# First feed-forward product by seven products of halves, in blocks 2 to 4 of a hybrid decoder layer

## The chip, the cores and the metric

The kernel runs on one core of one Trainium2 chip. The metric is the device time of one execution in microseconds. A core has five engines that run side by side, each with its own queue in order: TensorE (PE; its weight loads are shown apart as PEld), VectorE (DVE), ScalarE (ACT), GpSimd (POOL) and SyncE (SP), which issues nearly all DMAs here.

## The reference, cut to what matters

One layer over 2048 tokens of width 1024: a token mixer (gated DeltaNet, 8 heads) and a memory attention (4 heads) in parallel, an output projection, a layer norm, then a squared-ReLU MLP of width 4096 and a second layer norm. The change is in the MLP and in how weights reach it.

```python
x = layer_norm(ALPHA * x + mix, ln1_g, ln1_b)
x = layer_norm(ALPHA * x + sqrelu_mlp(x, w_ff1, w_ff2), ln2_g, ln2_b)

def sqrelu_mlp(x, w1, w2):
    return jnp.square(jax.nn.relu(x @ w1)) @ w2
```

All of it is in float32.

## The kernel before, in words

**Precision.** A float32 operand of a large product is written as a high part (rounded to fp32r, a cast on ScalarE) and a low part (the difference, a subtraction on VectorE): `split`, lines 460 to 462. A product is then three matmuls, high x high, high x low and low x high: `mm3`, lines 478 to 481. Weights are split where they are used.

**Blocks.** The 2048 tokens go in four blocks of 512 (the loop of line 1135; blocks are counted from 1 in this document, b = 0 in the code is block 1). In a block come, in this order: the mixer's projections, the mixer of each head and the memory attention (lines 1151 to 1162); the output projection in three parts of four heads (`out_proj`, lines 1165 to 1198, called with k0 = 0, 8 and 4), the last of which ends each of the four chunks of 128 tokens with its layer norm and its transposition into Thi and Tlo (`norm1`, `to_T`); the MLP (`ff_seven`, lines 1014 to 1093), whose last group also starts the next block.

**The MLP.** The 4096 hidden rows go in four groups g. The first product takes, per group, eight weight tiles of 128 hidden rows (`ff1_tiles`, lines 1216 to 1222): 8 k x 3 matmuls of 512 tokens each, in the accumulator tile "af". The first four tiles of a block run in halves of 256 tokens, so that they can start when the first two chunks are transposed. ScalarE applies relu and square; VectorE makes four sums of the quarters of the hidden tile, and all of it is split into the "xh" and "xl" slots (lines 1040 to 1060). The second product is already done by seven products of halves (Strassen's scheme in Winograd's form, table `SEVEN`, line 1010): sums of the hidden tile's quarters times sums of w_ff2's quarters. The latter are made once, in block 1, by `keep_sums` (lines 994 to 1006) and kept in DRAM as `tsc`, unsplit.

**Weights.** A raw weight of 512 KB is loaded into one of three 4 KB slots a partition ("wraw") and split into one of four 8 KB slots ("whl", high and low beside each other; lines 464 to 508). The weights of the mixer's projections are kept split in DRAM (`wsc`) from block 1 on and later loaded so.

**The order.** Everything is recorded first (`Recorder.add`) with the operations that it depends on and an estimated duration (`cost`, lines 190 to 226). `issue` (lines 228 to 333) then simulates the five queues and one DMA stream and gives each engine the ready operation with the lowest number (`prio`, its place in the program plus `shift`). A tile gets its slot in the order in which tiles are first used. The emitted order is fixed; on the chip every engine keeps to it. Each instruction stands under line 333, where the recorder emits it, so the profile is read by tile names.

Of the kernel before, what the change touches and what calls it, by code (L numbers as in the profile page):

```python
# [14 lines left out]
P = 128  # L15
TB = 512
# [123 lines left out]
class Recorder:  # L140
    def __init__(self, nc, tc):
        self.nc, self.tc, self.ops, self.shift = nc, tc, [], 0
# [9 lines left out]
    def add(self, eng, fn, name, args, kw):  # L152
        o = Op()
        o.i, o.eng, o.fn, o.args, o.kw = len(self.ops), eng, fn, args, kw
        o.succ, o.npred, o.ready, o.extra = [], 0, 0, 0
        o.prio = o.i + self.shift
        wr = [v for k, v in kw.items() if k in ("out", "accum_out")]
        rd = [v for k, v in kw.items() if k not in ("out", "accum_out")]
        rest = list(args)
        if "out" not in kw and rest:  # L160
            wr.append(rest.pop(0))
        rd += rest
        wr = [v for v in wr if isinstance(v, Ref)]
        rd = [v for v in rd if isinstance(v, Ref)]
        o.dur = self.cost(o, name, wr, rd, args, kw)
        o.p0 = tuple(r.p0 for r in wr[:1] + rd[:1])
        preds = {}
        for refs, is_w in ((rd, False), (wr, True)):
            for r in refs:
                for q, qw, qk in r.buf.log:  # L170
                    if (is_w or qw) and (qk is None or r.keys is None or qk & r.keys):
                        preds[q.i] = q
        for refs, is_w in ((rd, False), (wr, True)):
            for r in refs:
                log = r.buf.log
                if is_w:
                    log[:] = [e for e in log if not (e[2] == r.keys or r.keys is None)]
                log.append((o, is_w, r.keys))
        for q in preds.values():
            q.succ.append(o)  # L180
        o.npred = len(preds)
        o.bufs = list({id(r.buf): r.buf for r in rd + wr}.values())
        for b in o.bufs:
            if b.first is None:
                b.first = o.i
            b.users += 1
        self.ops.append(o)
# [162 lines left out]
def hybrid_layer(  # L350
# [39 lines left out]
    NW, NR = 4, 3  # L390
# [62 lines left out]
    inv = {}  # L453
    for n, f in (("LB", P), ("XB", P), ("L32", P), ("X32", P), ("X64", P), ("L64", P), ("Q", 64)):
        inv[n] = rec.buf(cst, (P, 2, f), F32, n, 1, n)
        nc.gpsimd.memset(inv[n], 0.0)
# [7 lines left out]
    def pair():  # L464

        t = rec.buf(wp, (P, 2 * 1024), F32R, "whl", NW, "whl")
        return t, t[:, :1024].part(*range(KT)), t[:, 1024:].part(*range(100, 100 + KT))

    def hilo(src, eng=None):
        t, hi, lo = pair()  # L470
        split(src, hi, lo, eng)
        return t, hi, lo
# [10 lines left out]
    def load_cols(w, u, eng=None):  # L483

        rt = rec.buf(wp, (P, 1024), F32, "wraw", NR, "wraw")
        nc.sync.dma_start(out=rt, in_=w[u])
        return as_cols(*hilo(rt, eng)[1:])
# [3 lines left out]
    def load_in(b, u):  # L491

        if b == 0:
            rt = rec.buf(wp, (P, 1024), F32, "wraw", NR, "wraw")
            nc.sync.dma_start(out=rt, in_=w_in[u])
            t, hi, lo = hilo(rt)
            nc.sync.dma_start(out=wsc[u], in_=t.bitcast(F32))
        else:
            t, hi, lo = pair()
            nc.sync.dma_start(out=t.bitcast(F32), in_=wsc[u])  # L500
        return as_cols(hi, lo)

    def load_rows(w, u, nh):

        rt = rec.buf(wp, (P, 1024), F32, "wraw", NR, "wraw")
        nc.sync.dma_start(out=rt, in_=w[u, nh])
        hi, lo = hilo(rt)[1:]
        return hi.rearrange("p (k f) -> p k f", k=2), lo.rearrange("p (k f) -> p k f", k=2)
# [6 lines left out]
    def layer_norm(y, g, b, dst=None):  # L515
# [8 lines left out]
        nc.gpsimd.tensor_tensor(out=rs, in0=ve, in1=mhalf[:, 0:1], op=ALU.pow)  # L524
        for i in range(2):
            c = slice(i * 512, (i + 1) * 512)
            yi = y[:, c].part(i)
            nc.vector.scalar_tensor_tensor(out=yi, in0=yi, scalar=mv[:, 0:1], in1=g[:, c],
# [18 lines left out]
    def T_tiles():  # L547
        return (rec.buf(tp, (P, KT, TB), F32R, "Thi", 1, "Thi"),
                rec.buf(tp, (P, KT, TB), F32R, "Tlo", 1, "Tlo"))

# [7 lines left out]
    def memory():  # L558
# [14 lines left out]
        for h in range(MH):  # L573
            w = load_cols(w_mem_k, h)
# [8 lines left out]
        for kk in range(4):  # L583
            w = load_rows(w_mem_v, kk, 0)
# [403 lines left out]
    def raw_rows(src):  # L988
        rt = rec.buf(wp, (P, 1024), F32, "wraw", NR, "wraw")
        nc.sync.dma_start(out=rt, in_=src)  # L990
        hi, lo = hilo(rt)[1:]
        return hi.rearrange("p (k f) -> p k f", k=2), lo.rearrange("p (k f) -> p k f", k=2)
# [16 lines left out]

    SEVEN = (("A11", "B11", "A", False, (0, 0)), ("S3", 3, "C", False, (1, 1)), ("S2", 2, "A", True, (1, 0)),  # L1010
# [3 lines left out]
    def ff_seven(b, ff1_tiles, relu2, add, norm2):  # L1014
        Q = 2 * P
        for g in range(NS):
# [3 lines left out]
            for v in range(2):  # L1020
                lo = [slot("xl", "s%d" % v, F32R) for _ in range(7)]
                hi = [slot("xh", "d", F32R) for _ in range(7 if v == 0 else 4)]
                if v:
                    hi += [hq[:, 0].part(0), hq[:, 1].part(1), slot("xh", "on", F32R)]
                sqs = [None, None]
                fs = [8 * g + 2 * v + o for o in (0, 4, 1, 5)]
                for part in ((0, 1, 2, 3),) if g == 0 and v == 0 else ((0,), (1,), (2,), (3,)):
                    if b == 0:
                        for j in range(2):
                            if 2 * j in part:  # L1030
                                keep_sums(u0 + v, j)
                    for i, a in zip(part, ff1_tiles([fs[i] for i in part], len(part) > 1)):
# [7 lines left out]
                        st = tok_tile("ss4")  # L1040
                        a11, a21, a12, a22 = (sq[:, q * Q:(q + 1) * Q] for q in range(4))
                        s = [st[:, q * Q:(q + 1) * Q].part(q // 2) for q in range(4)]
                        sub = lambda o, x, y, op=ALU.subtract: nc.vector.tensor_tensor(out=o, in0=x, in1=y, op=op)
                        sub(s[0], a21, a22, ALU.add)
                        sub(s[1], s[0], a11)
                        sub(s[2], a11, a21)
                        sub(s[3], a12, s[1])
                        h3, l3 = hi[3 * j:3 * j + 3], lo[3 * j:3 * j + 3]
                        two = lambda ap: ap.rearrange("p (i f) -> p i f", i=2)
                        split(sq.rearrange("p (j i f) -> p i j f", j=2, i=2)[:, 0], two(h3[0]), two(l3[0]))  # L1050
                        h22 = hi[6][:, j * Q:(j + 1) * Q].part(("x", j))
                        l22 = lo[6][:, j * Q:(j + 1) * Q].part(j)
                        split(a22, h22, l22)
                        for q in range(2):
                            split(st[:, q * TB:(q + 1) * TB].part(q), h3[1 + q], l3[1 + q])
                        x = {"A22": (h22, l22)}
                        for q, (n0, n1) in enumerate((("A11", "A12"), ("S1", "S2"), ("S3", "S4"))):
                            x[n0] = h3[q][:, :Q], l3[q][:, :Q]
                            x[n1] = h3[q][:, Q:], l3[q][:, Q:]
                        X[2 * v + j] = x  # L1060
# [5 lines left out]
            for n, (xn, wn, bn, on, (th, nh)) in enumerate(SEVEN[i] for i in order):  # L1066
# [4 lines left out]
                def part(t, v):  # L1071
                    if w[v] is None:
                        w[v] = raw_rows(tsc[u0 + v, wn] if wn in (1, 2, 3, 4)
                                        else w_ff2[u0 + v + (0 if wn == "B11" else 2), 1 if wn == "B22" else 0])
# [21 lines left out]
    def first_tokens():  # L1096
        T = T_tiles()
        rt = rec.buf(wp, (P, KT, P), F32, "wraw", NR, "wraw")
        wt, hi, lo = pair()
        hi, lo = hi.rearrange("p (k f) -> p k f", k=KT), lo.rearrange("p (k f) -> p k f", k=KT)  # L1100
# [12 lines left out]
        nc.sync.dma_start(out=wsc[0], in_=wt.bitcast(F32))  # L1113
# [21 lines left out]
    for b in range(NB):  # L1135
# [12 lines left out]
        for i in range(12):  # L1148
            cat_slot(i)
        r, A = {}, {}  # L1150
        for t in range(H + 2):
# [9 lines left out]
            if b == 0 and t == 0:  # L1161
                memory()
        ys = [None] * NC

        def out_proj(k0, tail=None):
# [11 lines left out]
            def part(t, nh, tag):  # L1177
                a = bank("ao", tag)
                for u in range(2):
                    if (u, nh) not in ws:  # L1180
                        ws[u, nh] = load_rows(w_out, k0 // 2 + u, nh)
# [12 lines left out]
            else:  # L1194
                for t in range(NC):
# [8 lines left out]
        T1 = T_tiles()  # L1204

        def norm1(t):
            layer_norm(ys[t], g1, b1)
            to_T(ys[t], T1[0], T1[1], t)
# [7 lines left out]
        def ff1_tiles(fs, halves):  # L1216

            wa = [(load_cols(w_ff1, f), bank("af", "m" if halves and i == 3 else "acc")) for i, f in enumerate(fs)]
            for t0, n in ((0, 256), (256, 256)) if halves else ((0, TB),):
                for w, a in wa:  # L1220
                    project(a[:, t0:t0 + n], w, T1, n, t0)
            return [a for _, a in wa]

# [14 lines left out]
        ff_seven(b, ff1_tiles, relu2, add, norm2)  # L1238
# [56 lines left out]
```

## Time and profile before

| | us |
|---|---|
| median of three runs | 2916.93 (2912.59 to 2917.21) |
| the profiled execution | 2914.94 |
| its span | 2913.2 |
| PE busy | 2862.8 |
| DVE busy | 2191.8 |
| ACT busy | 1527.1 |

The granted TensorE clock is 0.996 over the span. The profile gives busy time and idle time by engine and tile, the chain of work that ended last, and the DMA rate; it can be asked for any stretch of the span. Block 2 runs from about 785 to 1490 us, block 3 to about 2205 us; the MLP of block 2 begins at 1143.8 us.

### The profile page before, as it was taken

What the parts mean: (1) busy time and instruction counts of PE and PEld (TensorE: products, weight loads), DVE (VectorE), ACT (ScalarE), POOL (GpSimd) and SP (SyncE); (2) the same over time, 40 slices, a digit from 0 to 9 for tenths busy, and PEclk for the clock granted to TensorE, in tenths of its full rate; (3) what the DMA queues carried; (4) which work ended last, traced back from release to release, by engine and by line L of the source; (5) the groups of instructions that cost most, each with busy time, mean ns of one, the idle gap of its engine ahead of it and who ended that gap; (6) DMA issues with size and microseconds to landing.
All of it is one profiled execution on the core that took longest, in us unless ns stands there. A gap on an engine that the chain in (4) does not pass through costs nothing.

```text
span 2913.2 us, 42812 instructions
## 1 busy us (share of the span) xinstructions
PE 2862.8 (98%) x14404; PEld 2382.0 (82%) x14404; DVE 2191.8 (75%) x5762; ACT 1527.1 (52%) x3678; POOL 428.3 (15%) x1033
## 2 busy tenths in 40 slices
PE   8999999999999999999999999999999999999998
PEld 7888778888788878888878887888887888788886
DVE  7999987666888886665688887756668888676667
ACT  6677625454456653555536665344454666444443
POOL 2333210000133311000023321000001332000000
PEclk9999999999999999999999999999999999999999
DMA  7655567555743332544473333344456332234444
GB/s 278 251 201 203 191 228 236 190 193 182 266 151 139 122 105 81 159 143 134 157 256 138 138 116 105 92 147 145 152 176 226 141 138 98 98 94 151 146 145 137
DMA packets 127708, 469.79 MB, mean 161 GB/s; under 512 B 14464, under 2 KB 16896, under 8 KB 109056
## 3 DMA queue, kind: packets, MB, share of 16 engines
q1 hardware_dynamic: 126912, 467.00, 47.8%
q8 instruction: 114, 1.87, 0.3%
q14 instruction: 106, 0.87, 0.1%
q10 hardware_dynamic: 576, 0.06, 0.0%
HBM read 402.97 MB, written 64.03 MB: 160 GB/s over the span
## 4 chain that ended last, share of the span: by engine, by line
PE 81%; DVE 10%; DMA 4%; ACT 3%; issue 1%; POOL 1%; SPq 0%; ACTq 0%; POOLq 0%; DVEq 0%
PE af L333 39%; PE ao L333 7%; PE az L333 5%; PE av L333 5%; PE ak L333 5%; PE aq L333 4%; PE amq L333 3%; DVE y L333 3%; PE pc L333 3%; PE po L333 2%; DVE whl L333 2%; PE pkq L333 1%; PE pq L333 1%; PE pp L333 1%; DMA wq<-in_w_ff_dram 1%
## 5 line engine op out<-in xcount | busy, mean ns | idle before, releaser
L333 DVE TENSOR_TENSOR whl<-wraw,whl 128x1024 fp32r<-128x1024 f32 (+1 forms) x446 | 541.3, 1217 | 449.5 <-ACT whl L333 447.8
L333 PE MATMUL af<-Thi,whl 128*128 128x512 f32 (+1 forms) x2304 | 649.9, 366 | 5.1 <-DVE whl L333 3.9
L333 ACT CAST whl<-wraw 128x1024 fp32r<-128x1024 f32 (+1 forms) x446 | 466.8, 1047 | 355.3 <-PE af L333 208.6
L333 PEld LDWEIGHTS af<-Thi,whl 128*128 128x128 f32 x2304 | 416.6, 189 | 75.9 <-DVE whl L333 4.8
L333 PE MATMUL af<-whl,xh 128*128 128x512 f32 x1536 | 472.2, 390 | 0.0
L333 PE MATMUL af<-Tlo,whl 128*128 128x512 f32 (+1 forms) x1152 | 421.0, 366 | 0.0
L333 PE MATMUL af<-whl,xl 128*128 128x512 f32 x896 | 347.0, 390 | 2.3 <-DVE xl L333 2.3
L333 PEld LDWEIGHTS af<-whl,xh 128*128 128x128 f32 x1536 | 288.8, 188 | 61.2 <-ACT xh L333 0.5
L333 PE MATMUL ao<-whl,ch 128*128 128x512 f32 x768 | 253.2, 401 | 1.2 <-DVE y L333 1.2
L333 PEld LDWEIGHTS af<-Tlo,whl 128*128 128x128 f32 x1152 | 217.2, 189 | 35.1
L333 POOL TENSOR_SCALAR ve<-mv 128x1 f32<-128x1 f32 x34 | 22.5, 663 | 1513.6 <-DVE mv L333 1509.7
L333 ACT ACTIVATE rl<-af 128x512 f32<-128x512 f32 x128 | 76.5, 598 | 272.1 <-PE af L333 270.1
L333 PEld LDWEIGHTS af<-whl,xl 128*128 128x128 f32 x896 | 168.5, 188 | 37.7 <-DVE xl L333 2.8
L333 PE MATMUL aq<-Thi,whl 128*128 128x512 f32 x512 | 184.4, 417 | 6.8 <-ACT Thi L333 6.8
L333 PE MATMUL ak<-Thi,whl 128*128 128x512 f32 x512 | 175.9, 402 | 0.0
L333 PE MATMUL az<-Thi,whl 128*128 128x512 f32 x512 | 174.9, 402 | 0.0
L333 PE MATMUL av<-Thi,whl 128*128 128x512 f32 x512 | 174.5, 403 | 0.0
L333 PEld LDWEIGHTS ao<-whl,ch 128*128 128x128 f32 x768 | 142.6, 188 | 27.8 <-DVE y L333 2.1
L333 PE MATMUL ao<-whl,cl 128*128 128x512 f32 x384 | 154.8, 404 | 0.0
L333 DVE SCALAR_TENSOR_TENSOR y<-y,af 128x512 f32<-128x512 f32 x224 | 146.5, 679 | 8.9 <-PE af L333 8.9
L333 PEld LDWEIGHTS aq<-Thi,whl 128*128 128x128 f32 x512 | 94.1, 191 | 20.0 <-ACT Thi L333 6.8
L333 PEld LDWEIGHTS az<-Thi,whl 128*128 128x128 f32 x512 | 95.4, 188 | 17.0
(257 smaller groups left out, 5814.2 us busy)
## 6 DMA issues: line engine op xcount, KB each, us to landing
wraw<-in_w_ff_dram SPq DMA_DIRECT2D x224, 512.0 KB, 4.2
whl<-wsc SPq DMA_DIRECT2D x108, 1024.0 KB, 4.8
wraw<-tsc SPq DMA_DIRECT2D x128, 512.0 KB, 3.3
wsc<-whl SPq DMA_DIRECT2D x36, 1024.0 KB, 5.4
wraw<-in_w_out_dram SPq DMA_DIRECT2D x48, 512.0 KB, 3.6
wraw<-in_w_in_dram SPq DMA_DIRECT2D x35, 512.0 KB, 6.3
wq<-in_w_ff_dram SPq DMA_DIRECT2D x64, 256.0 KB, 4.2
tsc<-wq SPq DMA_DIRECT2D x64, 256.0 KB, 3.5
```

What stands on the lines that cost most here:

```text
L333: o.fn(*[res(a) for a in o.args], **{k: res(v) for k, v in o.kw.items()})
```

## The change

**The first product in blocks 2 to 4** (`ff1_quads`) takes eight groups v of 512 hidden rows. Of w_ff1's part for such a group, [1024 x 512], and of the block's tokens, [1024 x 512], it makes halves in both directions and computes seven products (table `FF1_SEVEN`), each as 2 x 4 x 3 matmuls of 256 tokens. The accumulators are read after each product, by copies on ScalarE and additions on VectorE, then relu, square, sums and splits as before. Block 1 keeps the plain product.

**The tokens' halves.** `to_quads` takes the place of `to_T` in these blocks: the last part of the output projection takes the chunks in the order 2, 3, 0, 1; B11 and B21 come from chunks 2 and 3, and when chunks 0 and 1 are there, VectorE makes T1 to T4 from both, which are split too. T1 lies in two weight slots.

**Weight parts in DRAM.** In block 1, the split quarters A11, A12 and A22 of w_ff1 are stored (`keep_parts`, 96 DMAs of 256 KB) and later loaded split; the sums S1 to S4 are made on VectorE (`ff1_sums`, 128 subtractions or additions of 256 columns) and stored unsplit (128 DMAs of 128 KB). The split w_out is stored too (`osc`) and loaded split in blocks 2 to 4. Three of four quarters of w_ff2 that the second product reads directly are copied within DRAM during block 1's mixer (`copy_rows`, 24 DMAs of 512 KB, each held until the operation recorded before it: `nc.after`) and read from the copies.

**One ring of slots.** Raw weights, high parts and low parts each take one 4 KB slot of eleven ("w", shown as wr, wh and wl). Where a weight isn't needed raw any more, it is loaded into its low part's slot and split in place (`hilo_in`).

**Also:** six tiles of the mixer's triangular inverse go from fixed memory to slots that are zeroed anew in each block; the hidden tile's splits go in smaller pieces, A11 and A22 first (`put`); `layer_norm` gets a variant that no call uses. The core of the diff:

```diff
-    NW, NR = 4, 3
+    NW = 11
...
+    def hilo_in(src):
+        t = unit("wl")
+        hi, lo = unit("wh").part(*HI), t.part(*LO)
+        nc.sync.dma_start(out=t.bitcast(F32), in_=src)
+        split(t.bitcast(F32), hi, lo)
+        return hi, lo
...
+    def load_hilo(src):
+        hi, lo = unit("wh").part(*HI), unit("wl").part(*LO)
+        for i, r in enumerate((hi, lo)):
+            nc.sync.dma_start(out=r.bitcast(F32), in_=src[:, 1024 * i:1024 * (i + 1)].part(i))
+        return hi, lo
...
+        Q["T1"] = [[unit("Tx", (P, 4, 256))] for _ in range(2)]
+        Q["T2"] = [[rec.buf(tp, (P, 4, 256), F32R, "kq1", 1, "Tx")],
+                   [rec.buf(tp, (P, 1, 256), F32R, "inv", 6, "Tx") for _ in range(4)]]
...
+    def to_quads(y, Q, keep, t):
...
+            if t >= 2:
+                quad_split(Q, ("B11", "B21")[j], t, pts[j])
+                f = v4(slot("tf", "d"))
+                nc.scalar.copy(out=f, in_=pts[j])
+                keep[t, j] = f
+        if t < 2:
+            nc.shift = 200 if t == 0 else 130
...
+            sub(s["T1"], b12, keep[t + 2, 0])
+            sub(s["T2"], b22, s["T1"])
+            sub(s["T3"], b22, s["B12"])
+            sub(s["T4"], keep[t + 2, 1], s["T2"])
+            quad_split(Q, "T2", t, s["T2"])
...
+    def copy_rows(u):
+        nc.after = nc.ops[-1]
+        for n in ("B11", "B21", "B22"):
+            nc.sync.dma_start(out=fcp[u, n], in_=w_ff2[u + (0 if n == "B11" else 2), 1 if n == "B22" else 0])
+        nc.after = None
...
+    FF1_SEVEN = (("A11", "B11", "A", False), ("A12", "B21", "B", False), ("S2", "T2", "A", True), ("S3", "T3", "C", False),
+                 ("S1", "T1", "A", True), ("A22", "T4", "C", True), ("S4", "B22", "A", True))
...
+    def keep_parts(f, hi, lo):
+        g, o = f // 8, f % 8
+        v, i = 2 * g + (o % 4) // 2, o % 2
+        for n, k in (("A11", 0), ("A12", 1)) if o > 3 else (("A22", 1),):
+            for h, r in enumerate((hi, lo)):
+                c = 1024 * h + 512 * i
+                nc.sync.dma_start(out=fhl[v, n][:, c:c + 512].part(h), in_=r[:, 512 * k:512 * (k + 1)].bitcast(F32))
...
+    def ff1_sums(f):
...
+            for n, x, y, op in (("S1", c1, c2, ALU.add), ("S3", a1, c1, ALU.subtract), ("S2", s["S1"], a1, ALU.subtract),
+                                ("S4", a2, s["S2"], ALU.subtract)):
+                nc.vector.tensor_tensor(out=s[n], in0=x, in1=y, op=op)
+                nc.sync.dma_start(out=fsc[v, n][:, 512 * j + 256 * i:512 * j + 256 * i + 256].part(2 * j + i), in_=s[n])
...
-                for t in range(NC):
+                for t in (2, 3, 0, 1) if b else range(NC):
...
+        def ff1_quads(vs, ACs, Bs, put):
...
+                wn, tn, bn, on = FF1_SEVEN[n]
+                if wn[0] == "A":
+                    hi, lo = load_hilo(fhl[v, wn])
+                else:
+                    hi, lo = hilo_in(fsc[v, wn])
...
+                    for k in range(4):
+                        th, tl = quad_k(T1, tn, k)
+                        for m, (a, x) in enumerate(((hi, th), (hi, tl), (lo, th))):
+                            first = start and k == 0 and m == 0
+                            nc.tensor.matmul(o.part(keys, other) if first else o.part(keys), a[:, i, k], x, start=first,
+                                             stop=k == 3 and m == 2, skip_group_check=True)
```

The first two products of the first two groups of a block are put ahead of the others in `ff1_quads`, since they need B11 and B21 only.

More of the change, by code (lines that the diff above doesn't have):

```diff
@@ new lines, in quad_split @@
+    def quad_split(Q, c, t, src):
+        h = t % 2
+        cols = slice(h * P, (h + 1) * P)
+        sub = []
+        for hl in range(2):
+            k = 0
+            for i, r in enumerate(Q[c][hl]):
+                n = r.shape[1]
+                sub.append((hl, k, n, r[:, :, cols].part((c, hl, h))))
+                k += n
+        his = [x for x in sub if x[0] == 0]
+        for _, k, n, r in his:
+            nc.scalar.copy(out=r, in_=src[:, k:k + n])
+        for _, k, n, r in sub:
+            if r not in [x[3] for x in his]:
+                for _, kh, nh, rh in his:
+                    a, b = max(k, kh), min(k + n, kh + nh)
+                    if a < b:
+                        nc.vector.tensor_tensor(out=r[:, a - k:b - k], in0=src[:, a:b], in1=rh[:, a - kh:b - kh].bitcast(F32),
+                                                op=ALU.subtract)
@@ L986, in hybrid_layer @@
            for g in range(NS) for u in (4 * g, 4 * g + 1) for i in range(1, 5)}
[L988 to L992, printed above, removed]
+    fcp = {(u, n): rec.buf(dr, (P, 1024), F32, "fcp%d_%s" % (u, n), 1, "fcp")
+           for g in range(NS) for u in (4 * g, 4 * g + 1) for n in ("B11", "B21", "B22")}
+    def copy_rows(u):
[3 more added lines that the diff above has]
+        nc.after = None
     def keep_sums(u, j):
```

289 lines of the change are left out of this document (227 added, 62 removed).

## The prediction

> **What bounds the kernel now.** I read the page first, then the matmuls by shape, then the waits on the chain, then stretches of block 1 (the first) and block 2, then the DMA rate.
>
> ```profile
> span 2913.2 us, 42812 instructions
> PE 2862.8 (98%) x14404; PEld 2382.0 (82%) x14404; DVE 2191.8 (75%) x5762; ACT 1527.1 (52%) x3678; POOL 428.3 (15%) x1033
> ...
> PE af L333 39%; PE ao L333 7%; PE az L333 5%; PE av L333 5%; PE ak L333 5%; PE aq L333 4%; PE amq L333 3%; DVE y L333 3%; PE pc L333 3%; PE po L333 2%; DVE whl L333 2%; PE pkq L333 1%; PE pq L333 1%; PE pp L333 1%; DMA wq<-in_w_ff_dram 1%
> ```
>
> TensorE is busy 98% of the span, and the tile "af", the accumulators of both feed-forward products, is 39% of the chain that ended last. A busy PE alone proves little, since matmuls overlap; so the stretches:
>
> ```profile
> core 0: us, PE busy (x) PEld busy (x) DVE busy (x) ACT busy (x) POOL busy (x), PEclk, DMA share, GB/s
> 20.00:30.00 10.00, 10.00 (x44) 8.28 (x45) 9.93 (x29) 5.15 (x10) 1.88 (x5) 1.00 1.01 418
> 80.00:90.00 10.00, 10.00 (x46) 8.26 (x45) 9.44 (x31) 5.67 (x9) 1.10 (x3) 1.00 1.03 414
> 340.00:480.00 140.00, 133.60 (x728) 111.97 (x726) 110.61 (x208) 58.91 (x124) 12.79 (x20) 1.00 0.68 227
> 520.00:560.00 40.00, 40.00 (x179) 33.10 (x178) 22.79 (x38) 20.97 (x33) 0.00 (x0) 1.00 0.56 182
> ...
> 1175.00:1300.00 125.00, 125.00 (x553) 103.52 (x552) 77.64 (x108) 62.03 (x84) 0.00 (x0) 1.00 0.47 144
> ```
>
> The last row lies in the feed-forward part of block 2: 553 matmuls of 128x512 in 125 us, no idle PE, granted clock 1.00, VectorE 62% busy, DMA at 144 GB/s. So there a matmul of 512 columns costs 125 / 553 = 0.226 us of the span, and only fewer TensorE columns shorten it. The pace of 256 columns is in the trace too, since the first four tiles of a block run in halves (timeline of PE):
>
> ```profile
> 1155.08 0.28 PE L333 MATMUL af<-Tlo,whl 128*128 128x256 f32 x1
> 1155.20 0.40 PE L333 MATMUL af<-Thi,whl 128*128 128x256 f32 x2
> ...
> 1161.56 0.28 PE L333 MATMUL af<-Tlo,whl 128*128 128x256 f32 x1
> ```
>
> One Tlo matmul and two Thi matmuls repeat every 0.36 us: 18 rounds from 1155.08 to 1161.56, 54 matmuls in 6.48 us, 0.120 us each, a little over half of 0.226.
>
> **TensorE in blocks 2 to 4.** Before, a block's first product is 32 tiles x 8 k x 3 matmuls; 28 tiles are 672 matmuls of 512 columns, four tiles are 192 of 256 columns: 672 x 0.226 + 192 x 0.120 = 151.9 + 23.0 = 174.9 us. After, eight groups x 7 products x 2 x 4 x 3 = 1344 matmuls of 256 columns: 161.3 us. That is 13.6 us less in a block and 40.8 us in three. One eighth of the columns goes (21.9 us), and the halves' worse pace gives part back. Transposes into the accumulators (8 banks a block) stay as many. This term is on the path, because nothing else ends a wait in the stretch above.
>
> **Feeding these products.** A weight is now used up in 24 x 0.120 = 2.9 us, formerly in 24 x 0.226 = 5.4 us. The second product already lives with 12 x 0.226 = 2.7 us a weight, with the same splits, in the same stretch without idle PE. Four of seven weights are still split on ScalarE and VectorE, as four of four before; three come as finished high and low parts, which doubles their bytes. Per block the first product loads 24 x 1.05 + 32 x 0.52 = 41.9 MB instead of 16.8 MB; the stretch's 144 GB/s becomes about 144 + 25.1 / 0.33 ms = 220 GB/s, half of the 418 seen. VectorE by its rows:
>
> ```profile
> L333 DVE TENSOR_TENSOR whl<-wraw,whl 128x1024 fp32r<-128x1024 f32 x443 | 539.7, 1222 | 449.1 <-ACT whl L333 447.4
> L333 DVE TENSOR_TENSOR xl<-ss,xh 128x512 fp32r<-128x512 f32 x96 | 61.8, 684 | 0.0
> L333 DVE TENSOR_TENSOR ss<-sq 128x256 f32<-128x256 f32 x128 | 48.2, 418 | 0.0
> L333 ACT CAST xh<-ss 128x512 fp32r<-128x512 f32 x96 | 59.4, 622 | 49.5 <-DVE ss L333 49.5
> ```
>
> For each of 32 blocks of hidden rows come three more additions of 256 (PSUM in; taken at 0.418 us) and one more split piece, about 1.4 us; a group of 81 us holds four, so 62% of 125 us becomes about 75% of a shorter stretch. ScalarE gives its 512-wide pairs up for 11 pieces of 256 and was 50% busy. The w_out splits (12 x 1.222 us) leave blocks 2 to 4; VectorE was not the limit there, so that is worth nothing. The single ring of eleven 4 KB slots replaces three raw slots and four 8 KB pairs, the same 44 KB; a split weight that is loaded into its own low slot takes two slots instead of three, and two slots are lent to T1 for the whole feed-forward part: 9 / 2 = 4.5 weights in flight, formerly three raw and four split. I take zero, covered by the idle 38% of VectorE and the DMA's margin; without that cover a stall shows as PE waiting on "wl".
>
> **The start of the first product in blocks 2 to 4.** Here work is added just where little covers it:
>
> ```profile
> 1143.55 0.39 PE L333 MATMUL ao<-whl,cl 128*128 128x512 f32 x1
> 1143.78 0.28 PE L333 MATMUL af<-Thi,whl 128*128 128x256 f32 x1
> ...
> 1149.09 0.50 PE L333 MATMUL af<-Thi,whl 128*128 128x256 f32 x2 [0.93 <-DVE whl L333]
> ...
> 1153.02 0.60 PE L333 MATMUL pt<-ident,y 128*128 128x128 f32 x4
> 1153.38 0.36 PE L333 MATMUL af<-Thi,whl 128*128 128x256 f32 x1
> 1153.58 0.28 PE L333 MATMUL af<-Tlo,whl 128*128 128x256 f32 x1
> 1153.70 0.60 PE L333 MATMUL pt<-ident,y 128*128 128x128 f32 x4
> ```
>
> The last out-projection matmul starts at 1143.55, and the last token chunk is transposed at 1153.02 to 1154.1, some 10 us later. The four half tiles cover that: 96 x 0.120 = 11.5 us. After, chunks 2 and 3 come first, and the first two products of two groups need only them: 4 x 24 x 0.120 = 11.5 us of cover again. Then product S2 x T2 needs the last chunk after two subtractions on VectorE (0.68 each by the xl row of 512 columns), a cast on ScalarE (0.62 by the xh row) and four splits of 128 columns (0.3 each, an estimate from 0.418 for 256): 10.5 + 1.4 + 0.6 + 1.2 = 13.7 us against 11.5 + 1.1 us of transposes: 1 us short, if VectorE is free. It is not quite:
>
> ```profile
> 1147.82 1.21 DVE L333 TENSOR_TENSOR whl<-wraw,whl 128x1024 fp32r<-128x1024 f32 x1
> 1148.95 0.68 DVE L333 TENSOR_TENSOR Tlo<-pt,Thi 128x512 fp32r<-128x512 f32 x1
> 1149.55 0.20 DVE L333 BATCH_NORM_AGGREGATE mv<-bn 128x2 f32<-128x12 f32 x1
> 1149.66 1.17 DVE L333 TENSOR_TENSOR whl<-wraw,whl 128x1024 fp32r<-128x1024 f32 x1
> 1150.75 1.41 DVE L333 SCALAR_TENSOR_TENSOR y<-y,mv,l1g 128x512 f32<-128x512 f32 x2
> ```
>
> These follow each other without a gap. Four weight splits (4.8 us) leave this stretch, since the first four weights arrive split; for each of chunks 0 and 1 come four subtractions and three more splits, 2 x 7 x 0.68 = 9.5 us. Behind a late VectorE instruction queue the weight splits and accumulator reads of the next five products. Net 4.7 us of VectorE at worst lands on the path: bounds 0 (all of it behind later products) and 8 us (that plus the 1 us and two weight splits). I take 3 us less the 0.93 us that goes: 2 us a block, 6 us in all.
>
> **Block 1 pays for the stores.** It keeps its plain first product and gains these DMAs: 12 w_out weights x 2 x 0.52 = 12.6 MB; 96 pieces of 256 KB of split w_ff1, 25.2 MB; 128 pieces of 128 KB of its sums, 16.8 MB, made by 128 additions of 0.418 us on VectorE. The first product of one group is 8 x 24 x 0.226 = 43.4 us and receives 10.5 MB of that, 242 GB/s on top of the 182 GB/s of the row 520 to 560: 424 GB/s, where 418 is the best that any stretch shows. VectorE there rises from 22.8 of 40 us (57%) to about 88%. The first 140 us (row 340 to 480) hold 31.8 MB and get 12.6 + 10.5 MB: 54.9 MB, 392 GB/s. SyncE issues all of it in order, 0.33 us and more each:
>
> ```profile
> 454.54 2.03 SPq L333 DMA_DIRECT2D wraw<-in_w_ff_dram  x2
> 460.33 1.52 SPq L333 DMA_DIRECT2D tsc<-wq  x3
> 462.67 0.33 SPq L333 DMA_DIRECT2D wraw<-in_w_ff_dram  x1
> ```
>
> A store that waits for its sum holds up the weight loads queued behind it, and a raw slot stays taken until the sums have read it. Lower bound 0 (418 GB/s reached, the rest moved into the second product's quieter stretches). Upper bound: at the rate per share of the row 340 to 480, 227 / 0.68 = 334 GB/s, three groups take 18.4 / 0.334 = 55 us instead of 43.4 and the first stretch 164 instead of 140: 3 x 11.7 + 24 = 59 us. I take 3 us a group, 12 us, near the lower end, because the rows at 414 and 418 GB/s also mix stores with loads.
>
> **Copies of w_ff2 in block 1's first stage.** 24 copies, DRAM to DRAM, 12.6 MB read and written. The stretch from 100 to 340 us (its columns: us, PE busy, clock, DMA share, GB/s):
>
> ```profile
> 100.00:340.00 240.00, 238.23 (x1334) 1.00 0.56 198
> ```
>
> 198 GB/s becomes 198 + 25.2 / 0.24 = 303 GB/s: hidden on average, but a load behind a burst of three lands later. I take 3 us, bounds 0 and 10. Six memsets a block on GpSimd (15% busy) cost nothing.
>
> **The sum.** The profiled execution took 2914.9 us (span 2913.2 plus 1.7). 2914.9 - 40.8 + 6 + 12 + 3 = 2895 us. The median of the shown runs lies 2 us above that execution: 2897 us. A measurement of this kernel can tell about 0.2%, 6 us, from no change.
>
> **Rivals.**
> 1. All additions hide: 2916.9 - 40.8 - 2 (the small stall goes too) = 2874 us. For it: a planner that knows durations orders everything and PE is idle only 50 us now. Against it: DMA and VectorE demands near full in block 1.
> 2. Slower: block 1's first product becomes bound by DMA. The mechanism is the 424 GB/s of demand; it decides as soon as block 1 loses over 32 us (40.8 less the 9 us above), that is at a sustained rate of about 365 GB/s: there a group takes 50.4 us (7 more) and the first stretch 150 (10 more). At the bound of 334 GB/s: 2916.9 - 40.8 + 9 + 59 = 2944 us. For it: stores of 128 and 256 KB, in order on one queue. Against: 414 GB/s.
> The Trainium skill, "DMA: Bandwidth & Descriptors", section Specifications, states a limit of about 358 GB/s of HBM for one core; by that rule the groups cost 3 x 8 and the first stretch 13 us, 37 us in all, and the time is 2922 us. The rows at 414 and 418 GB/s do not agree with it as a limit here.
> 3. VectorE is late at each start by 8 us, or halves run slower than 0.120 us (0.130 us would eat the whole gain): 2916.9 - 40.8 + 24 + 15 = 2915 us, no change. Against: the 54 matmuls at 0.120.
>
> **How the numbers follow.** Forecast 0.52 (2883 to 2909), rival 1 0.18 (2868 to 2883), rival 2 0.20 (2912 to 2944), rival 3 0.10. Faster by over 0.2% (below 2911): 0.50 + 0.18 + 0.02 = 0.70. Within 0.2%: 0.02 + 0.02 + 0.05 = 0.09. Slower: 0.18 + 0.03 = 0.21. The range 2870 to 2935 leaves out a little of rivals 1 and 2. The likely case's own range is 2883 to 2909.
>
> **What would show it.** Right: 1344 af matmuls of 128x256 in a block's first product at 0.120 us; blocks 2 to 4 some 11 us shorter each; block 1 longer by 10 to 20 us with DMA above 350 GB/s in its first products. Wrong: block 1 longer by over 40 us with PE waiting for weights behind stores; PE idle before T2 or T3 by over 5 us a block; PE waiting on "wl" between the products.

## The result, and the profile after

The changed kernel takes 2948.97 us (median of four runs, 2939.32 to 2952.39), the kernel before 2917.07 in the same comparison (2912.59 to 2921.43). The ratio is 1.0104, 95% interval 1.0075 to 1.0133: slower by 1%, where 2897 us and a range up to 2935 were forecast. The profiled execution took 2947.32 us (before 2914.94).

The page of the changed kernel, its first lines and the DMA totals (helper line 335 is the former 333; wr, wh and wl are the slots of the ring, Tx the parts of T1, T2 and T4):

```profile
span 2945.6 us, 47726 instructions
PE 2847.1 (97%) x15844; PEld 2427.8 (82%) x15844; DVE 2289.4 (78%) x6128; ACT 1590.8 (54%) x4087; POOL 426.0 (14%) x1051
DMA packets 210870, 631.62 MB, mean 214 GB/s; under 512 B 24000, under 2 KB 42816, under 8 KB 210240
```

TensorE is busy 15.7 us less than before, yet the span is 32.4 us longer. Its idle time went from 50.4 to 98.5 us. The chain of the new page covers only its last pieces, so it answers nothing; the table of stretches does. First the kernel before, then the changed one (columns as in the prediction's rows: us, PE busy and its matmuls, granted clock, DMA share, GB/s). In each, the first row runs from the first gate transfer to block 1's first MLP matmul, the second to the start of block 2, the third to block 2's first MLP matmul, the fourth to the start of block 3:

```profile
38.50:425.10 386.60, 377.45 (x2037) 0.99 0.63 219
425.10:780.40 355.30, 349.28 (x1632) 1.00 0.64 211
780.40:1143.50 363.10, 360.32 (x1932) 1.00 0.36 126
1143.50:1492.20 348.70, 346.98 (x1632) 1.00 0.51 162
```

```profile
38.40:435.50 397.10, 382.10 (x2037) 0.98 0.78 277
435.50:817.40 381.90, 358.92 (x1631) 0.97 0.88 304
817.40:1179.70 362.30, 359.72 (x1933) 1.00 0.44 145
1179.70:1530.50 350.80, 338.68 (x2114) 1.00 0.69 232
```

Block 1 ends 37.0 us later: 10.5 us come before its first product (first rows), 26.6 in the MLP (second rows). There the same matmuls have 23.0 us of idle time beside them instead of 6.0, and take 9.6 us more themselves, at a clock of 0.97. Block 2, where the change was to save, is 1.3 us longer, though TensorE is busy 8.3 us less in its MLP: the saving is there and idle time has eaten it. Taken in the same way, block 3 went from 713.4 to 712.5 and block 4 from 707.3 to 702.3. The sum is 37.0 + 1.3 - 0.9 - 5.0 = 32.4 us, the whole difference (the marks between the blocks are good to about 0.3 us).

**Block 1.** Its waits from 436 to 810 us in the changed kernel (engine, who waited for whom: total us, times, longest):

```profile
ACT wh L335 <- DMA wr<-in_w_ff_dram: 55.7, 25, 6.1
DVE fs L335 <- DMA wr<-in_w_ff_dram: 35.9, 13, 5.4
ACT wh L335 <- DMA wl<-tsc: 29.4, 20, 3.8
...
ACT wh L335 <- DMA wl<-fcp: 14.7, 15, 2.6
...
PE af L335 <- ACT xh L335: 9.2, 3, 3.9
...
PE af L335 <- ACT wh L335: 7.0, 2, 6.0
```

and before, from 425 to 775 us:

```profile
ACT whl L333 <- DMA wraw<-tsc: 12.9, 8, 2.9
...
ACT whl L333 <- DMA wraw<-in_w_ff_dram: 2.0, 2, 1.7
```

ScalarE's casts of weights wait 100 us for their loads instead of 15. Most of that costs nothing. It costs at the start of the second product, where pieces of the hidden tile (xh) queue behind a cast that waits. The changed kernel's longest stop, in its timelines of PE, ScalarE and SyncE's queue (start, us):

```profile
490.10 0.39 PE L335 MATMUL af<-wh,xl 128*128 128x512 f32 x1
496.53 1.22 PE L335 MATMUL af<-wh,xh 128*128 128x512 f32 x2 [6.04 <-ACT wh L335]
...
498.38 0.63 PE L335 MATMUL af<-wh,xl 128*128 128x512 f32 x1
498.80 0.63 PE L335 MATMUL af<-wh,xh 128*128 128x512 f32 x1
499.23 0.63 PE L335 MATMUL af<-wl,xh 128*128 128x512 f32 x1
```

```profile
488.67 0.63 ACT L335 ACTIVATE sq<-rl 128x512 f32<-128x512 f32 x1 [3.07 <-DMA tsc<-wq]
...
495.43 1.04 ACT L335 CAST wh<-wl 128x1024 fp32r<-128x1024 f32 x1 [2.28 <-DMA wl<-fcp]
496.38 0.61 ACT L335 CAST hq<-ss 128x512 fp32r<-128x512 f32 x1
496.90 0.40 ACT L335 CAST xh<-ss 128x256 fp32r<-128x256 f32 x1
```

```profile
487.52 0.62 SPq L335 DMA_DIRECT2D fhl<-wl  x1
488.19 1.76 SPq L335 DMA_DIRECT2D fsc<-fs  x2
489.99 1.60 SPq L335 DMA_DIRECT2D wl<-fcp  x2
```

The weight's load was issued at 489.99, behind stores of parts and sums, and its cast could start at 495.43, 5.4 us later. TensorE waited 6.04 us for it, and two more pieces of the hidden tile stood behind that cast. The last three PE rows show a second price: the matmuls follow each other in 0.43 us instead of 0.226 for some 4 us after the stop. The other three stops of over 2 us in this MLP (3.2, 2.2 and 3.9 us) also begin within 7 us of the start of a second product; there TensorE waits for a piece xh whose relu and square came behind such casts. The DMA rate around such places (changed kernel; us, PE, PEld, DVE, ACT, POOL, clock, DMA share, GB/s):

```profile
460.00:470.00 10.00, 10.00 (x65) 9.08 (x64) 7.22 (x18) 8.00 (x15) 0.00 (x0) 1.00 1.02 335
487.00:498.00 11.00, 4.92 (x19) 3.27 (x18) 7.77 (x16) 5.65 (x10) 0.00 (x0) 0.83 1.00 345
500.00:510.00 10.00, 9.44 (x39) 7.38 (x38) 8.65 (x11) 3.61 (x4) 0.00 (x0) 0.95 1.03 402
540.00:550.00 10.00, 10.00 (x46) 8.29 (x45) 7.70 (x17) 6.09 (x10) 0.00 (x0) 1.00 1.01 368
```

The rows of 10 us are three of 17 such stretches in block 1's MLP with a DMA share of 0.98 or more. Those moved 335 to 402 GB/s, 362 on the mean: full, below the 414 and 418 of the prediction's rows.

**Blocks 2 to 4.** A steady group of block 2's first product, changed kernel (nine rows out of a timeline of all engines):

```profile
1273.50 0.28 PE L335 MATMUL af<-Thi,wl 128*128 128x256 f32 x1
...
1273.62 0.28 PE L335 MATMUL af<-Thi,wh 128*128 128x256 f32 x1
...
1273.74 0.28 PE L335 MATMUL af<-Tlo,wh 128*128 128x256 f32 x1
...
1273.86 0.28 PE L335 MATMUL af<-Thi,wl 128*128 128x256 f32 x1
1274.25 0.42 DVE L335 TENSOR_TENSOR sq<-sq,af 128x256 f32<-128x256 f32 x1 [1.32 <-ACT wh L335]
1274.59 1.22 DVE L335 TENSOR_TENSOR wl<-wl,wh 128x1024 fp32r<-128x1024 f32 x1
...
1274.72 0.19 PEld L335 LDWEIGHTS af<-Thi,wh 128*128 128x128 f32 x1 [0.79 <-DVE sq L335]
1274.73 0.39 PE L335 MATMUL af<-Thi,wh 128*128 128x256 f32 x1 [0.58 <-DVE sq L335]
...
1274.95 0.28 PE L335 MATMUL af<-Tlo,wh 128*128 128x256 f32 x1
```

The pace is 0.12 us as predicted. Then a step of 0.87 us. The group's first matmul starts at 1269.31, so its 36th, at 1273.50, is the last into the first half of accumulator B, and the three after it go into the second half. VectorE reads the first half at 1274.25, and the next weight load and matmul into the second half are released by that read. VectorE was not late through other work: it had been idle for 1.32 us, though the half was done at 1273.78, and the weight's split comes behind the read. The read starts 0.11 us after the third of those matmuls ends (1273.86 + 0.28), so it was ordered behind them and ahead of the fourth. (The cast printed as its releaser is the last of several waits.) The 0.87 us are the end of one matmul, 0.42 us of reading and the handing over. TensorE's waits in block 2's MLP, changed kernel (1179.7 to 1474 us):

```profile
PE af L335 <- ACT sq L335: 4.4, 6, 1.8
PE af L335 <- DVE sq L335: 3.8, 7, 0.6
PE af L335 <- DVE tq L335: 1.5, 1, 1.5
PE af L335 <- DVE wl L335: 1.3, 1, 1.3
```

and before, in the same part:

```profile
PE af L333 <- DVE whl L333: 0.9, 1, 0.9
```

"sq" is the read of an accumulator. These reads, more than weights, hold TensorE up. Block 2 has eight stops at VectorE's reads (the eighth just behind this stretch), of 0.79 to 0.86 us from matmul to matmul, 5.6 us beyond the pace in all. Before each, VectorE stood idle, and it began within 0.11 us of the end of the last matmul. Of the six stops at ScalarE's reads two (3.2 us beyond the pace) came late, behind casts of the hidden tile. Block 2's four first products took 47.7, 43.5, 43.5 and 43.5 us before (from first matmul to the second product's first) and take 51.2, 42.9, 43.5 and 42.7 now, where 336 matmuls at 0.120 are 40.3. The second product kept its 38.1 us.

### The profile page after: what moved, and what is told of

The parts are those of the page before. It is cut to its first block, busy times and chain, and to the rows that moved or that the text cites. A ratio compares the mean times of both kernels' runs of the same rounds, so it can differ in the third digit from the quotient of the medians.

```text
span 2945.6 us, 47726 instructions
## 1 busy us (share of the span) xinstructions
PE 2847.1 (97%) x15844; PEld 2427.8 (82%) x15844; DVE 2289.4 (78%) x6128; ACT 1590.8 (54%) x4087; POOL 426.0 (14%) x1051
## 5 line engine op out<-in xcount | busy, mean ns | idle before, releaser
L335 ACT CAST wh<-wl 128x1024 fp32r<-128x1024 f32 x320 | 335.2, 1049 | 351.7 <-DMA wl<-fsc 104.4
L335 DVE TENSOR_TENSOR wl<-wl,wh 128x1024 fp32r<-128x1024 f32 x320 | 387.2, 1221 | 139.5 <-ACT wh L335 137.8
L335 PE MATMUL af<-wh,xl 128*128 128x512 f32 x896 | 351.4, 393 | 0.2 <-DVE xl L335 0.2
L335 PE MATMUL af<-Thi,wh 128*128 128x256 f32 (+1 forms) x1056 | 325.5, 309 | 10.0 <-DVE sq L335 5.3
L335 PE MATMUL af<-Thi,wl 128*128 128x256 f32 (+1 forms) x1056 | 324.6, 308 | 10.2 <-DVE wl L335 6.6
L335 PE MATMUL af<-Tlo,wh 128*128 128x256 f32 (+1 forms) x1056 | 325.0, 308 | 6.0 <-DVE sq L335 4.6
L335 PE MATMUL af<-wh,xh 128*128 128x512 f32 x768 | 299.6, 393 | 16.2 <-ACT xh L335 9.2
L335 PE MATMUL af<-wl,xh 128*128 128x512 f32 x768 | 301.9, 393 | 1.4 <-DVE wl L335 1.3
L335 PE MATMUL af<-Tx,wh 128*128 128x256 f32 x1152 | 212.1, 285 | 10.7 <-ACT sq L335 10.5
L335 PEld LDWEIGHTS af<-Thi,wh 128*128 128x128 f32 x1056 | 202.5, 192 | 23.3 <-DVE sq L335 7.1
```

Of the source, the lines that this page charges most:

```text
L335: o.fn(*[res(a) for a in o.args], **{k: res(v) for k, v in o.kw.items()})
```

## The experiments

The theory: the stores starve block 1; in blocks 2 to 4 the token sums at the start and the reads between halves eat the saving. The rivals: VectorE's additions, not the stores, delay block 1; weights come late in blocks 2 to 4; the ring of slots costs time by itself. Ratios are against the kernel before, run beside each.

**Without stores and sums of w_ff1.**

```diff
-                    keep_parts(f, hi, lo)
...
-                if f % 8 > 3:
-                    ff1_sums(f)
...
-                    hi, lo = load_hilo(fhl[v, wn])
...
+                        nc.sync.dma_start(out=r.bitcast(F32), in_=wsc[(4 * v + n) % 36][:, 1024 * h:1024 * h + 1024].part(h))
...
-                    hi, lo = hilo_in(fsc[v, wn])
+                    hi, lo = hilo_in(tsc[4 * (v // 2) + v % 2, 1 + n % 4])
```

> Block 1 makes and stores no part and no sum of w_ff1; blocks 2 to 4 load the same number of bytes from other tiles kept in DRAM, so their products have other values. Theory (the stores fill the DMA queue, weight loads land late, ScalarE's casts wait for them in order and the start of each second product in block 1 waits for ScalarE): the four second-product stretches of block 1, now 47.3, 43.0, 42.3 and 50.3 us, return to about 42, 38, 38 and 42, and the time falls from 2949 to about 2925 us; blocks 2 to 4 stay as they are. Rival (the order that the planner emits for block 1 is longer whatever the DMAs do): less than 8 us.

Measured: 2927.25 us, ratio 1.0037 (1.0024 to 1.0050), 22 us below the changed kernel. Block 1 ends at 791.7 instead of 817.4 us; its second products take 45.5, 38.1, 38.1 and 42.6 us, so only the first of them stays long.

**The sums made, but not stored:** as above, with `ff1_sums` kept and its DMA line taken out.

> As the run without stores, but the 128 additions of w_ff1's sums stay on VectorE in block 1, their results unused. Theory (DMA): within 4 us of the run without sums and stores, about 2925 us. Rival (VectorE's 54 us of additions delay block 1): 2940 us or more, the second-product stretches of block 1 stay long.

Measured: 2921.35 us, ratio 1.0020 (1.0008 to 1.0033), 28 us below the changed kernel. The additions on VectorE cost nothing; the stores do. Block 1's two stretches (as in the tables above):

```profile
38.10:436.50 398.40, 382.13 (x2037) 0.98 0.77 274
436.50:787.40 350.90, 347.52 (x1629) 1.00 0.64 213
```

The MLP of block 1 is back from 381.9 to 350.9 us, its idle time from 23.0 to 3.4 us, its clock to 1.00. The stretch ahead of it is as long as before the edit. ScalarE's casts still wait 83 us for their loads here (34.9, 29.0 and 18.6 by tensor), so that total says little by itself; what went are TensorE's own waits in this part, from 21.1 to 2.9 us.

**A's two halves in one bank and C's in another, each accumulator read when both its halves are done:**

```diff
-                        o = ACs[v, i][:, 256 * (bn == "C"):256 * (bn == "C") + 256]
-                        keys, other = bn, "C"
...
+                    full = Bs[v] if bn == "B" else ACs[v, int(bn == "C")]
+                    o, keys, other = full[:, 256 * i:256 * i + 256], (bn, i), (bn, 1 - i)
...
-                    reads.append((v, n, i, o.part(keys)))
+                    reads.append((v, n, i, o.part(keys, other)))
```

> The two i halves of accumulator A share one PSUM bank and those of C another (A and C of one i shared one before), and a read waits for both halves. Theory (a read of one half of a bank is ordered between two matmuls into the other half, and TensorE stands still for the drain and the read, 0.67 us each, some 2.5 us a group): the first-product stretches of groups 2 to 4 in blocks 2 to 4 fall from about 42.9 to about 40.5 us, and the time from 2949 to about 2925 us. Rival (the readers are simply late, since ScalarE and VectorE are busier): stretches stay above 42 us and the time within 6 us of 2949.

Measured: 2984.65 us, ratio 1.0240 (1.0222 to 1.0258): a clear miss. Its waits of PE in block 2's MLP:

```profile
PE af L335 <- DVE wl L335: 5.0, 5, 1.3
PE af L335 <- ACT sq L335: 4.8, 2, 4.5
PE af L335 <- ACT wh L335: 2.3, 3, 1.5
PE af L335 <- DVE tq L335: 1.7, 1, 1.7
```

VectorE's reads no longer stop TensorE. But now all reads come at the end of a product: one stop of 4.5 us in the first group, and weights that are split too late. The first group takes 54.3 us at a clock of 0.94, and the last second product 46.7 instead of 42.2. Curing one wait everywhere made others.

**A11, A12 and A22 loaded raw and split in every block**, no stores of parts:

```diff
-                    keep_parts(f, hi, lo)
...
-                    hi, lo = load_hilo(fhl[v, wn])
+                    t = unit("wr", dt=F32)
...
+                    hi, lo = hilo(t)
```

> Block 1 stores no split quarters of w_ff1 (25 of the 42 MB of stores go); blocks 2 to 4 load A11, A12 and A22 raw from w_ff1 and split them, 24 more splits a block. Theory (DMA stores in block 1): about 12 us less, 2937 us, and the first products of blocks 2 to 4 not longer by over 1 us each. Rival (the sums and their small stores are what costs): the second-product stretches of block 1 stay, 2945 us or more.

Measured: 2968.60 us, ratio 1.0182 (1.0166 to 1.0197), where 2937 was expected: a miss. Block 1 gains 22 us (it ends at 795.6 instead of 817.4), but blocks 2 to 4 take 727.3, 727.4 and 717.6 us, about 14 to 15 us more each, for 24 more splits a block. PE's waits for "wl" in block 2's MLP go from 1.3 to 5.8 us and the second product from 38.1 to 39.8. So storing the split parts costs 22 us in block 1 and spares some 44 us behind it: of these two ways it is the better one.

**No stored w_out, no copies of w_ff2** (both loaded raw):

```diff
-                        w[v] = as_rows(*hilo_in(tsc[u0 + v, wn] if wn in (1, 2, 3, 4) else fcp[u0 + v, wn]))
+                        w[v] = as_rows(*(hilo_in(tsc[u0 + v, wn]) if wn in (1, 2, 3, 4) else
+                                         hilo(load_raw(w_ff2[u0 + v + (0 if wn == "B11" else 2), 1 if wn == "B22" else 0]))))
...
-                copy_rows(4 * ((t - 1) // 2) + (t - 1) % 2)
...
-                        ws[u, nh] = load_out(b, k0 // 2 + u, nh)
+                        ws[u, nh] = load_rows(w_out, k0 // 2 + u, nh)
```

> w_out isn't kept split in DRAM (it is split in every block, as before) and no part of w_ff2 is copied in DRAM; all else as in the changed kernel. Theory (DMA in block 1): the first product of block 1 starts at about 426 instead of 435.5 us, the second-product stretches of block 1 stay long, and the time is about 10 us lower, 2939 us. Rival (the ring of eleven slots makes block 1 late): the start stays at 433 us or more.

Measured: 2953.60 us, ratio 1.0139 (1.0120 to 1.0158); another miss. Block 1's first product starts at 429.9 instead of 435.5 and the block ends 7 us earlier; blocks 2 to 4 give it back with 714.3, 718.3 and 708.6 us, and two of the four second products of each take 39.9 us instead of 38.1. A copied quarter is split in place and takes two slots instead of three; the run leaves out the stored w_out along with the copies, so what each of them is worth is not shown apart.

**Without the token sums** (T1 to T4 are not made, B11 and B21 take their places):

```diff
-            sub(s["T1"], b12, keep[t + 2, 0])
...
-            quad_split(Q, "T4", t, s["T4"])
...
+                        th, tl = quad_k(T1, {"T1": "B11", "T2": "B21", "T3": "B11", "T4": "B21"}.get(tn, tn), k)
```

> T1 to T4 aren't made: the products S1, S2, S3 and A22 take B11 or B21 in their place, so their values differ; the matmuls and the weights are the same. Theory (the making of T1 to T4 on VectorE and ScalarE holds up the first group of each of blocks 2 to 4): its first-product stretch falls from 51 to 53 us to about 44 us, and the time by about 24 us to 2925 us. Rival (the late reads of the second group's accumulators set that stretch): it stays at 49 us or more and the time within 8 us of 2949.

Measured: 2935.57 us, ratio 1.0068 (1.0053 to 1.0083). That is 13 us less than the changed kernel: the first groups take 47.9, 52.2 and 48.1 us instead of 51.2, 53.0 and 51.3. The direction is right, the size half of what was expected. In the profiled executions it is 8.7 us, 7.3 of them in these three groups.

**Reads of B wait for both halves:**

```diff
-                    reads.append((v, n, i, o.part(keys)))
+                    reads.append((v, n, i, o.part(keys, other) if bn == "B" else o.part(keys)))
```

> Only the reads of accumulator B wait for both of its halves; A and C stay as in the change. Theory (a read ordered into the matmuls of the other half of its bank stops TensorE for 0.67 to 0.74 us): the stops of VectorE's B reads vanish from the middle of these streams, once or twice a group, steady stretches fall by about 1 us, and the time by 8 to 15 us to about 2937 us. Rival (stops only move, since the reads or the weight splits come later): steady stretches stay at 42.5 to 43.5 us and the time at 2945 us or more.

Measured: 2937.91 us, ratio 1.0077 (1.0062 to 1.0092), 11 us less. The steady groups take 41.1 to 43.3 us, most of them 41.1 to 42.1. With the stops at B gone, part of the saving of a group shows. The four executions of the changed kernel spread over 13 us, so the single effects of 13 and 11 us are each good to some 9 us only.

**The other edits alone:** plain products in all blocks, with the ring of eleven slots, the splits in place, the hidden tile's smaller pieces and the inverse tiles in slots; no parts or sums of w_ff1, no stored w_out, no copies.

> The seven products, the stores, the kept w_out and the copies are all left out: what stays of the change is the ring of eleven 4 KB slots, in-place splits of loaded sums, the smaller hidden-tile splits and the inverse's tiles in slots. Theory (these edits cost and bring nothing): within 6 us of the kernel before, 2917 us. Rival (the ring itself costs): 2925 us or more.

Measured: 2904.63 us, ratio 0.9965 (0.9954 to 0.9975): faster than both kernels. Its blocks take 745.1, 709.0, 708.3 and 705.4 us (before 741.9, 711.8, 713.4 and 707.3, each from the gate transfer on). So these edits bring some 10 us (6.4 in the profiled executions, 2908.55 for 2914.94), and the rest of the change costs some 42.

**Known costs off together:** no stores of w_ff1, no token sums, B read after both halves.

> The changed kernel with three edits of earlier runs together: block 1 makes its sums of w_ff1 but stores neither them nor the split parts, so blocks 2 to 4 load the same number of bytes of other data; the token sums T1 to T4 aren't made, the products take B11 and B21 in their place; reads of the accumulator B wait for both halves. Output is not the reference's. My theory, that these are separate costs: 2949 - 28 (stores) - 13 (token sums) - 11 (reads between the halves) = 2897 us. Rival, that one cost showed three times (all three starve the same few places): no better than 2915 us, since e2_sums_no_stores alone gave 2921. A third, that all of the predicted 41 us is there once the costs are off: 2917 - 41 = 2876 us or less.

Measured: 2894.99 us, ratio 0.9927 (0.9910 to 0.9944), 2 us from the sum of the three single effects and 20 from the rival. They are separate costs. Against the run that leaves out the stores alone (2921.35), the token sums and the reads of B are 26.4 us together, and there the executions lie far apart (2893 to 2896 and 2916 to 2931). PE's waits in block 2's MLP:

```profile
PE af L335 <- DVE sq L335: 2.1, 4, 0.5
PE af L335 <- ACT sq L335: 1.8, 4, 0.5
```

Its four first products take 46.2, 41.7, 41.7 and 41.8 us. The third expectation, all of the 41 us, falls: eight reads still stop TensorE in this part, and the first group stays 6 us over 40.3.

**And no stored w_out or copies:**

```diff
-            keep_hilo(osc[u, nh], hi, lo)
+            hi, lo = load_hilo(wsc[2 * u + nh])
...
-                copy_rows(4 * ((t - 1) // 2) + (t - 1) % 2)
...
+            hilo_in(tsc[u0 + v, wn if wn in (1, 2, 3, 4) else 1])
```

> As e12_four_costs_off, and block 1 also neither stores the split w_out nor copies w_ff2 in DRAM; blocks 2 to 4 load the same number of bytes from other tensors, so their work is the same, with other data. Output is not the reference's. My theory, that these stores and copies delay the start of block 1's first product by the 10 us seen there (435.5 for 425.1 us): 10 us less than e12_four_costs_off, about 2887 us, all of it in block 1. Rival, that this delay has another cause (the ring of slots): within 3 us of e12_four_costs_off.

Measured: 2889.21 us, ratio 0.9909 (0.9894 to 0.9924). That is 6 us less, but not where it was expected: block 1 ends at 788.6 us, with the edit before at 787.1, and its first product still starts at 433.5. The gain lies in blocks 2 to 4 (703.5, 703.2 and 694.2 us for 705.4, 705.1 and 696.2). So the late start of block 1's first product is only in part due to these transfers. It is 429.9 and 429.5 in the two kernels with raw w_ff2 and w_out, and 425.1 before; what makes up the rest stays open.

## Why the prediction was wrong

The sum forecast a difference of -40.8 + 6 + 12 + 3 = -19.8 us on the profiled execution; it is +32.4. The miss of 52.2 us splits by the same steps.

**"TensorE in blocks 2 to 4", right.** Over 300 of the 336 matmuls of a group follow the one before in 0.12 us. TensorE is busy only 8.3 us less in block 2's MLP, not 13.6, since at each stop the end of the last matmul (0.28 us against the pace of 0.12) and a slower step behind it count as busy.

**"Feeding these products" and "The start of the first product", wrong: 40.4 us of the miss.** The first products of blocks 2 to 4 take 180.3, 181.8 and 178.1 us, for 178.2 in each before: +5.6 us in all where -34.8 was forecast. The step that failed is the zero for feeding, with the 2 us for the start. The prediction looked for late weights and counted each new accumulator read as VectorE time (1.4 us of additions and splits for each of four blocks in a group; that makes 16 in a block of tokens, where its text says 32), covered by a VectorE that is idle 38%. But a read is not only work: the next matmul waits for it. Two times seven products on two halves give 28 reads a group where eight tiles gave eight. Most of this is not the lateness of a full engine: VectorE was idle before each of its eight reads that stopped TensorE in block 2. The read is ordered between two matmuls into the same bank, and TensorE stands still for it, 0.67 to 0.74 us beyond the pace. The signs named were only half right: PE's wait for "wl" is 1.3 us in block 2, the waits for "sq" 8.2. Shown by experiment are 13 us for the token sums and 11 for the reads of B (26 for both together); with both gone the first products of blocks 2 to 4 take 171.4, 171.8 and 171.6 us, 20 us less than before, half of the 40.8. The other 15 us of the miss are gaps that remain with both off. The waits left in block 2 (3.9 us) all lie at accumulator reads, most likely those of A and C; that was not shown, since the kernel that moved those reads lost more elsewhere.

**"Block 1 pays for the stores" and "Copies", too small: 22.0 us of the miss.** 15 us were taken, 37.0 measured, inside the bounds of 0 and 69. The value was put near the lower end because of the rows at 414 and 418 GB/s. Those rows say what the DMA engines reached there, not that every load lands in time. At a share of about 1 the stretches of block 1's MLP got 335 to 402 GB/s, and loads came late in ScalarE's order. The stores alone are 28 us of the time and 31 of block 1's MLP.

**The w_out splits that go, "worth nothing", and the ring, "zero": 10.2 us on the other side.** Blocks 2 to 4 together are 4.6 us shorter though their first products are 5.6 longer, so the rest of them gained 10.2. The plain products in the new ring gain 9.8 us in these blocks without the stored w_out, 6.5 of them outside the first products. So most of it comes from what that run keeps (the ring, the splits in place, the smaller pieces, the inverse's slots); which of these does it was not tried, and the other 4 us stay open. The balance is 40.4 + 22.0 - 10.2 = 52.2.

**The rivals.** Rival 2 gave the sign and 2944 us, but it was right for half a reason. Block 1 did lose more than the 32 us from which it was to decide, 37.0. But its first-product stretches, which it had put 11.7 us longer, take 51.8, 43.5, 43.5 and 44.8 us, up to 2.4 more than before. Most of the loss is in the second product, 47.6, 43.2, 42.5 and 50.3 us for about 43, 38, 38 and 42: here demand beyond the rate was paid less where it arose than by the loads queued behind it. And rival 2 still counted on the saving in blocks 2 to 4. The rule of the Trainium skill that stood with it ("DMA: Bandwidth & Descriptors", Specifications, about 358 GB/s for one core) gave an estimate of 2922 us; a stretch of 10 us at 402 GB/s does not agree with it as a limit, though it lies nearer to the mean of these full stretches, 362, than 418 does. Rival 3 had VectorE late by up to 8 us at each start; the first groups took 3.5, 5.3 and 3.6 us longer than before, and the halves kept to 0.120 us but for 13 matmuls at 0.21 in block 3, where the granted clock was 0.51.

## What to carry to other kernels

When a product is cut into more and smaller ones, count the reads of accumulators and ask of each which matmul waits for it, even where the reading engine is idle, and what stands ahead of it on that engine; a cheaper product whose results are read three times as often can give all of its saving back. Traffic that is added to one stage in order to save in others is to be priced by what is queued behind it in that stage (here casts in ScalarE's order, then hidden-tile pieces, then TensorE), not by the mean rate against the best rate seen. And where a change bundles several edits, run the plain ones alone: here they were the gain.

## What the runs showed of the hardware

**A stop costs TensorE twice.** After the 6.04 us stop of block 1 the 512-column matmuls follow each other in 0.43 us instead of 0.226 for about 4 us, and the stretch from 487 to 498 us has a granted clock of 0.83. Over block 1's MLP the same matmuls are busy 9.6 us longer, most of it in such stretches, beside 17.0 us of added idle time. The Trainium skill, "TensorE: Matmul & The Clock Gate", section "What's actually happening", says that the array falls to half its clock after an idle window of about 3.4 us and comes back after about as long of sustained work; the 0.43 us agrees with half the clock. The 3.4 us of idle time do not hold as a condition here: a stop of 2.15 us (669.0 to 671.1) was followed by a granted clock of 0.50 from 671.7 to 675.1, and in block 3 stops of 0.46 and 1.30 us between 1911.6 and 1914.6 went with one of 0.51 from 1914.1 to 1917.5. The stops of the steady group shown above, all under 1 us, left it at 1.00:

```profile
1269.00:1311.90 42.90, 41.35 (x338) 40.46 (x336) 26.85 (x47) 30.74 (x65) 0.00 (x0) 1.00 0.68 227
```

**Halves of an accumulator bank were not independent.** The order written for this kernel treats the two halves as separate tiles, yet a matmul into one half started only after the read of the other, at 0.87 us instead of 0.12. Reading B only when both halves were done took 11 us off. In the trace this is a wait of the program: the weight load at 1274.72 is released by a semaphore that the read raises. Whether the chip could do without that wait was not tried.

**Full is not one rate.** The DMA share was 1.02 at 335, 1.00 at 345, 1.01 at 368 and 1.03 at 402 GB/s in block 1's MLP, and 1.01 at 418 in a stretch near the start of the kernel before.
